# Hymba block on one core: split queries and keys stored interleaved, scan streams stored block by block, and a new order

## The chip, the cores and the metric

The kernel runs on one core of one Trainium2 chip. The metric is the device time of one execution in microseconds (us); less is better. Each core has a matrix engine (TensorE, PE in the profile), a vector engine (VectorE, DVE), an activation engine (ScalarE, ACT), a general engine (GpSimd, POOL), a queue engine that only issues transfers (SyncE, SP), and 16 DMA engines which all queues share. Transfers are issued here from SP, from POOL, and a few from ACT.

## The reference, cut to what matters

One layer over 1024 tokens of width 1024, all in float32: a SwiGLU FFN, a mixer, and a second FFN, each with a norm before and behind it. The mixer projects a token into an attention part and an RWKV part, computes both and projects their outputs back.

```python
f = _swiglu(_rmsnorm(h, ffn1_pre_g[l]), ffn1_w_gate[l], ffn1_w_up[l], ffn1_w_down[l])
h = h + 0.5 * _rmsnorm(f, ffn1_post_g[l])
z = _rmsnorm(h, mix_pre_g[l]) @ w_in[l]
y_att = _attention_group(z[..., :ATT_IN], cos, sin, attn_out_g[l])
y_rwkv = _rwkv7_group(z[..., ATT_IN:], ...)
mix = jnp.concatenate([y_att, y_rwkv], axis=-1) @ w_out[l]
h = h + _rmsnorm(mix, mix_post_g[l])
f = _swiglu(_rmsnorm(h, ffn2_pre_g[l]), ffn2_w_gate[l], ffn2_w_up[l], ffn2_w_down[l])
h = h + 0.5 * _rmsnorm(f, ffn2_post_g[l])
```

The attention has 8 heads of 64 features with rotary positions; each query sees three dilated windows of keys, (128, 1), (512, 4) and (2048, 16). The RWKV part has 8 heads; each runs a recurrence with a 64 x 64 state over the tokens, once forward and once backward, and the two results are added:

```python
sa = jnp.einsum('dbhvk,dbhk->dbhv', state, kk)
state = state * w[..., None, :] - sa[..., :, None] * kka[..., None, :] + v[..., :, None] * k[..., None, :]
y = jnp.einsum('dbhvk,dbhk->dbhv', state, r)
```

## The kernel before, in words

**Split numbers.** TensorE multiplies a rounded form of float32 (F32R) quickly. Where the kernel needs more precision it splits a value into a high part h and a low part l (`split`: h by an ACT copy, l by a VectorE subtraction) and adds three or four products of parts.

**Stages.** FFN 1; projection of the low-rank inputs and the RWKV columns (`project_rwkv`, tiles zr); projection of keys, queries and values by tokens (`project_tokens`, tiles zq, in the order keys, queries, values); attention head by head (`attention`) mixed with the scan over 8 blocks of 128 tokens in both directions (`prep`, `solve`, `merge`, `chain`); the end of the mixer in 8 units (`finish_unit`) with the output projection; FFN 2. Nothing is held in the code's order: the whole program is recorded on a tape first, and the order is worked out for each engine (below).

**Queries and keys.** For each of 8 token tiles and each half of the heads, and for queries as for keys, `project_tokens` (L930) multiplies, rotates, and turns a [128, 2, 128] tile in PSUM (zt). ACT writes its high part (zth) and a full copy (zts), VectorE its low part (ztl); each has two buffers. Three POOL transfers put them into three DRAM tensors of [4 pairs of heads, 128, 1024]: q_d or kt_d, each with f, h and l. For a head, `stacked` (L1121) loads three tiles of 128 partitions with two half loads each (64 partitions): sq is query h over query l, kh is key h twice, kl is key l twice. `scores` inside `near` (L1142) adds sq x kh and sq x kl, which are the four products of parts. The full copies serve the widest window (`far`), a pair of heads at a time.

**Streams of the scan.** Decay and rate (w and a, one for each direction) come from `low_rank` (L997), the streams r, k, kk and v from `stream` (L1032). All lie in DRAM as [features / 128, 128, 1024]: a partition's 1024 tokens are one 4 KB row. `prep` (L1246) loads of each of them 128 tokens of all rows (tiles th_w, th_a and in3), forms the block's operands and writes the block's keys (d_kd) in the same layout; `chain` writes the block's outputs (d_y), from ACT's queue. `finish_unit` (L1442) loads 256 tokens of two rows of y and keys in both directions, r and v.

**Inverses.** `solve` (L1316) loads a block's matrix X from DRAM, runs 31 steps of two small operations (ttmp, Ti) on POOL for blocks 1 to 5 and on VectorE for the others, and stores the result (d_t, d_tt) from POOL; `merge` loads it back from POOL (tiles d, tt) for PE's products pa and pb.

**What sets the order.** `_Tape.cost` (L257) prices each operation: `took` is how long it holds its engine, `late` how long the result takes after that, `moved` the time on the DMA wire. `sweep` (L345) plays the program with these prices, engine by engine, always taking the ready operation of lowest rank; `order` (L460) runs sweeps forward and backward, keeps the best, then adds to the ranks of some ranges of operations the amounts of the table LEADS (45 entries) and sweeps once more. `play` (L486) issues the result; all operations therefore have L491 in the profile, and groups are told apart by the names of their tiles.

Of the kernel before, what the change touches and what calls it, by code (L numbers as in the profile page):

```python
# [11 lines left out]
F32 = mybir.dt.float32  # L12
F32R = mybir.dt.float32r
# [19 lines left out]
def _ap(src, off, pat):  # L33
# [66 lines left out]
class _Tape:  # L100
# [156 lines left out]
    def cost(self, op):  # L257
# [8 lines left out]
        if op.method == "dma_start":  # L266
            runs = [math.prod(q[1] for q in a.ap) // (a.ap[-1][1] if a.ap[-1][0] == 1 else 1) for a in (x, *op.ins)]
            size = math.prod(q[1] for q in x.ap) * 4
            half = any(a.tensor.name in self.home and a.ap[0][1] <= 64 for a in (x, *op.ins))
            op.took, op.late = (560 if op.eng == "gpsimd" else 360) + 200 * half, 1500 + (600 if half else 0)  # L270
            op.moved = (14 * max(runs) + 0.0384 * size) / 16
        elif op.eng == "tensor":
# [14 lines left out]
            op.late = 170  # L287
        elif op.eng == "vector":
# [8 lines left out]
            op.took, op.late = 150 + rate * n + (83 if "accum_out" in op.kwargs else 0), 35  # L297
            op.port = sum(self.home.get(a.tensor.name, (None,))[0].space is None for a in op.ins
                          if a.tensor.name in self.home and math.prod(q[1] for q in a.ap[1:]) > 1) > 1
            if op.method == "reciprocal":  # L300
                op.took = 150 + 5 * n
        elif op.eng == "scalar":
            func = op.args[2] if op.method == "activation" else None
            aps = sum(isinstance(op.kwargs.get(k), bass.AP) for k in ("scale", "bias"))
            op.took = 170 + 0.87 * n + 95 * aps + (188 if "accum_out" in op.kwargs else 0)
            op.load, op.late = LOADS.get(func, 0), 40
        else:
            op.took, op.late, op.port = (200 + 2.1 * n if op.method != "memset" else 130 + 0.8 * n), 40, op.method != "memset"

    def pace(self, last, op, idle):  # L310
# [4 lines left out]
        return took + 95 if last and last.grid != op.grid and idle < 100 else took  # L315

    def lag(self, p, s):

        if p.eng is None or p.eng == s.eng and p.method != "dma_start":
            return 0.0  # L320
        return p.late + p.moved + (200 if s.eng == "gpsimd" else 0)
# [23 lines left out]
    def sweep(self, back=False):  # L345
# [29 lines left out]
        follow, last, port = None, None, 0.0  # L375
        while True:
# [26 lines left out]
            while op is None and heap[e]:  # L403
# [5 lines left out]
                if tag:  # L409
# [5 lines left out]
                    if at > t + 1e-6:  # L415
                        push(later[e], (at, -op.rank, op.n, op))
                        op = None
                        continue
                    slots[tag].remove(at)
# [15 lines left out]
            if op.port:  # L435
                t = max(t, port)
                port = t + took
# [3 lines left out]
            if op.moved and not back:  # L441
                wire = max(wire, own) + op.moved
                end = wire - op.moved
            op.end = end
# [191 lines left out]
class _Kernel:  # L636
# [293 lines left out]
    def project_tokens(self, p, psum, x):  # L930

        nc, V, A, G, T = self.nc, self.nc.vector, self.nc.scalar, self.nc.gpsimd, self.nc.tensor
        for b, g in [(b, g) for b in (1, 0, 2) for g in range(2)]:
            hl = self.columns(p, b * 512 + g * 256, 256)
            for t in range(NT):
# [23 lines left out]
                for d, src in zip((self.q_d, self.kt_d)[b], (y, h, l)):  # L959
                    G.dma_start(d[g * 2:g * 2 + 2, :, ts].rearrange("a p t -> p a t"), src[:].bitcast(F32))  # L960
# [36 lines left out]
    def low_rank(self, ring, rows, psum, nm, y, reset):  # L997
# [6 lines left out]
        for d in range(2):  # L1004
# [11 lines left out]
            for pr in range(4):  # L1016
# [13 lines left out]
                self.nc.sync.dma_start(self.lr_d[nm][d][pr], o)  # L1030

    def stream(self, p, psum, ct, y):  # L1032
# [8 lines left out]
        elif ct < 4:  # L1041
            self.nc.gpsimd.dma_start(self.rk_d[ct], y)
        elif ct < 8:
            i = ct - 4
            self.nc.gpsimd.dma_start(self.rk_d[4 + i], y)
# [20 lines left out]
            self.nc.gpsimd.dma_start(self.rk_d[8 + i], kr)  # L1066
# [54 lines left out]
    def stacked(self, p, h):  # L1121

        ds = slice(h % 2 * 64, h % 2 * 64 + 64)
        (_, qh, ql), (_, kh, kl) = self.q_d, self.kt_d
# [8 lines left out]
    def near(self, psum, p, h, sq, kh, kl, v, far, between):  # L1133
# [8 lines left out]
        def scores(t):  # L1142
# [61 lines left out]
    def attention(self, psum, p):  # L1204
        X, F, ST = {}, {}, {}

        def load(pr):
# [7 lines left out]
            self.load(q, self.q_d[0][pr])  # L1215
            self.load(k, self.kt_d[0][pr])
# [29 lines left out]
    def prep(self, n, p, psum, big):  # L1246
# [4 lines left out]
        ls = slice(n * TB, (n + 1) * TB)  # L1251
# [3 lines left out]
        for d in range(2):  # L1255
            b = n if d == 0 else NC_ // BLK - 1 - n
            ts = slice(b * TB, (b + 1) * TB)
# [631 lines left out]
```

## Time and profile before

| | |
|---|---|
| median of 3 runs | 2257.74 us (2257.31 to 2260.61) |
| profiled execution | 2272.18 us, span 2270.4 us |
| PE busy | 2175.3 us, 96% of the span |
| VectorE, ACT, POOL busy | 1519.2, 1051.3, 720.1 us |
| mean granted PE clock | 0.970 |
| DMA | 408.71 MB, mean 180 GB/s |
| DMA pieces | 373,053, of which 279,282 are under 2 KB |

In the profile a row such as `kh<-d_kth SPq DMA_DIRECT2D` is a transfer into tile kh from DRAM tensor d_kth, issued by SP. Tensor and tile names are given without their numbers, so that in3 is shown as in, s12 as s and h1_d as d_h. A row of the table of stretches has the stretch, its length, then for PE, PE's weight loads, VectorE, ACT and POOL the busy time and in brackets the number of instructions, then PE's granted clock, the busy share of the 16 DMA engines, and GB/s. A PE that is busy at a granted clock of 0.5 works at half speed; busy time alone doesn't show it. In a table of single transfers the last number is the median time from issue to landing in us.

### The profile page before, as it was taken

To read this page: it belongs to the slowest core of one execution; us is meant where nothing else is said; L and a number is where in the kernel's file an instruction comes from. 1 tells how busy PE (TensorE), PEld (TensorE's weight loads), DVE (VectorE), ACT (ScalarE), POOL (GpSimd) and SP (SyncE) were. 2 spreads that over 40 slices of the span, in tenths; PEclk is the share of its full clock that TensorE was granted. 3 is DMA by queue.
4 is the path that set the end of the run, shared out by engine and by line. 5 is a ranking of instruction groups with operands and counts; after the bars stand their busy time and mean duration, and the time that the engine had idled before them with its cause. 6 is when DMAs were issued, how large, how long until landed. Compare 5 with 4: busy or idle time off the path is not lost.

```text
span 2270.4 us, 41200 instructions
## 1 busy us (share of the span) xinstructions
PE 2175.3 (96%) x15236; PEld 1799.2 (79%) x15236; DVE 1519.2 (67%) x2630; ACT 1051.3 (46%) x2023; POOL 720.1 (32%) x1038
## 2 busy tenths in 40 slices
PE   7999999999999999998989998898899999999998
PEld 5888888888887888898768777666688888888886
DVE  8877777775685477562635557647978777787566
ACT  6333333354576464543546566454533333335453
POOL 2244444520000010667373571221024444443000
PEclk9999999999999999999969799998999999999999
DMA  5355444586662377764967765587435544458665
GB/s 153 115 170 165 163 152 163 185 289 194 202 201 83 115 252 197 213 206 143 231 159 183 164 160 149 136 274 252 151 108 177 168 156 160 147 181 299 198 203 182
DMA packets 373053, 408.71 MB, mean 180 GB/s; under 512 B 76658, under 2 KB 279282, under 8 KB 372852
## 3 DMA queue, kind: packets, MB, share of 16 engines
q1 hardware_dynamic: 324096, 303.18, 45.2%
q0 software_dynamic: 30704, 94.44, 11.9%
q10 hardware_dynamic: 18052, 8.46, 1.4%
q8 instruction: 120, 1.97, 0.4%
q14 instruction: 81, 0.66, 0.1%
HBM read 271.69 MB, written 134.28 MB: 179 GB/s over the span
## 4 chain that ended last, share of the span: by engine, by line
PE 81%; DMA 6%; DVE 5%; POOL 2%; issue 2%; ACT 2%; SPq 1%; DVEq 0%; ACTq 0%; POOLq 0%
PE gu L491 37%; PE pd L491 17%; PE zr L491 5%; PE zq L491 5%; PE po L491 3%; PE pt L491 2%; PE lp L491 2%; DVE row L491 2%; PE s L491 2%; PE xu L491 2%; POOL Ti L491 1%; PE y L491 1%; POOL ttmp L491 1%; SPq L491 1%; DMA X<-d_x 1%
## 5 line engine op out<-in xcount | busy, mean ns | idle before, releaser
L491 ACT ACTIVATE wh<-raw 128x512 fp32r<-128x512 f32 x264 | 162.8, 628 | 373.5 <-PE gu L491 276.4
L491 POOL TENSOR_TENSOR row<-row 128x512 f32<-128x512 f32 x88 | 129.3, 1469 | 447.6 <-DVE row L491 420.2
L491 DVE TENSOR_TENSOR row<-gu,row 128x512 f32<-128x512 f32 x308 | 203.5, 685 | 101.1 <-PE gu L491 63.1
L491 DVE TENSOR_TENSOR wl<-raw,wh 128x512 fp32r<-128x512 f32 x264 | 214.5, 823 | 82.3 <-ACT wh L491 57.9
L491 PE MATMUL gu<-xh,wh 128*128 128x512 f32 x704 | 249.9, 394 | 3.6 <-ACT xh L491 1.5
L491 PE MATMUL gu<-xh,wl 128*128 128x512 f32 x704 | 250.6, 391 | 0.6 <-DVE wl L491 0.6
L491 PE MATMUL gu<-xl,wh 128*128 128x512 f32 x704 | 249.5, 393 | 0.0
L491 DVE TENSOR_TENSOR gwl<-graw,gwh 128x512 fp32r<-128x512 f32 (+1 forms) x176 | 116.4, 664 | 107.5 <-PE pd L491 76.0
L491 PE MATMUL pd<-gh,gwl 128*128 128x512 f32 x616 | 180.9, 391 | 0.5 <-DVE gwl L491 0.5
L491 PE MATMUL pd<-gl,gwh 128*128 128x512 f32 x616 | 180.0, 390 | 0.2 <-DVE gl L491 0.2
L491 PE MATMUL pd<-gh,gwh 128*128 128x512 f32 x616 | 180.2, 390 | 0.0
L491 ACT ACTIVATE gwh<-graw 128x512 fp32r<-128x512 f32 (+1 forms) x176 | 101.0, 577 | 137.0 <-PE pd L491 113.2
L491 PEld LDWEIGHTS gu<-xh,wh 128*128 128x128 f32 x704 | 132.9, 189 | 32.8 <-ACT xh L491 2.1
L491 PEld LDWEIGHTS gu<-xh,wl 128*128 128x128 f32 x704 | 132.3, 188 | 28.6 <-DVE wl L491 1.2
L491 PEld LDWEIGHTS gu<-xl,wh 128*128 128x128 f32 x704 | 132.6, 189 | 27.4 <-DVE xl L491 0.5
L491 PEld LDWEIGHTS pd<-gh,gwl 128*128 128x128 f32 x616 | 115.6, 188 | 25.3 <-DVE gwl L491 0.9
L491 PEld LDWEIGHTS pd<-gl,gwh 128*128 128x128 f32 x616 | 115.5, 188 | 24.7 <-DVE gl L491 0.6
L491 PEld LDWEIGHTS pd<-gh,gwh 128*128 128x128 f32 x616 | 115.5, 188 | 24.0
L491 ACT ACTIVATE gh<-raw 128x512 fp32r<-128x512 f32 x160 | 99.4, 629 | 57.0 <-PE pd L491 34.2
L491 DVE TENSOR_TENSOR gl<-raw,gh 128x512 fp32r<-128x512 f32 x160 | 115.7, 729 | 11.4 <-ACT gh L491 10.9
L491 POOL TENSOR_TENSOR ws<-ws 128x512 f32<-128x512 f32 x88 | 118.8, 1351 | 2.8
L491 POOL DMA_DIRECT2D d_hid<-row x154 | 83.8, 547 | 81.6 <-DVE row L491 67.6
(300 smaller groups left out, 5149.9 us busy)
## 6 DMA issues: line engine op xcount, KB each, us to landing
d_hid<-row POOLq DMA_DIRECT2D x154, 256.0 KB, 2.7
graw<-d_hid SPq DMA_DIRECT2D x132, 256.0 KB, 3.1
raw<-in_ffn_w_gate_dram SPq DMA_DIRECT2D x88, 256.0 KB, 3.0
raw<-in_ffn_w_up_dram SPq DMA_DIRECT2D x88, 256.0 KB, 3.1
ws<-in_ffn_w_down_dram SPq DMA_DIRECT2D x88, 256.0 KB, 3.7
d_ws<-ws POOLq DMA_DIRECT2D x88, 256.0 KB, 2.8
raw<-d_ws SPq DMA_DIRECT2D x88, 256.0 KB, 3.2
raw<-in_ffn_w_down_dram SPq DMA_DIRECT2D x66, 256.0 KB, 4.1
```

What stands on the lines that cost most here:

```text
L491: i = getattr(getattr(self.nc, op.eng), op.method)(*op.args, **op.kwargs).ins
```

## The change

**Interleaved split queries and keys.** The high and the low part are written into one tile w of [128, 2, 2, 128]. A new DRAM tensor kk holds, for each head, 64 features x (h, l) x 1024 tokens, so that 128 rows of 4 KB are one head. Queries have two such tensors: q1 with h before l, q2 with l before h. `stacked` loads three whole tiles for a head, and the scores are q1 x kk + q2 x kk: the same four products. A tile of keys now needs three POOL transfers (the full copy and two halves of w), a tile of queries five.

**Streams block by block.** w, a, the three streams, the written keys and the outputs lie in DRAM as [8 blocks, 128, rows, 128 tokens]. `prep` and `chain` move a partition's part of a block in one run; `low_rank` and `stream` write their 1024-token rows in 8 pieces of 128 tokens; `finish_unit` loads each stream but v in two transfers, since two blocks and two rows don't make one simple pattern.

**The order.** The prices of `cost`, the lags between operations and the pace of PE when its shape changes are other formulas; transfers have at most 8 in flight for each kind of queue in `sweep`; LEADS has 19 other entries. Every engine's order changes with that, also in the FFNs.

The diff, cut to its core (the new LEADS table is left out):

```diff
             size = math.prod(q[1] for q in x.ap) * 4
-            half = any(a.tensor.name in self.home and a.ap[0][1] <= 64 for a in (x, *op.ins))
-            op.took, op.late = (560 if op.eng == "gpsimd" else 360) + 200 * half, 1500 + (600 if half else 0)
-            op.moved = (14 * max(runs) + 0.0384 * size) / 16
+            rows = min(a.ap[0][1] for a in (x, *op.ins) if a.tensor.name in self.home)
+            op.took, op.late = 360 + 200 * (rows <= 64), 1700
+            if op.eng == "gpsimd":
+                op.took = 560 + 0.25 * max(runs)
+            runs = 6 * size / 4096 if op.eng == "gpsimd" else max(size / 4096, *runs)
+            op.moved = max((9.5 * runs + 0.0366 * size) / 16, size / (3.6 * rows))
...
-            op.late = 170
+            op.late = 200
...
-            op.took, op.late = 150 + rate * n + (83 if "accum_out" in op.kwargs else 0), 35
+            op.took, op.late = 68 + rate * n + 65 * (len(op.ins) > 2), 117
...
-            op.took = 170 + 0.87 * n + 95 * aps + (188 if "accum_out" in op.kwargs else 0)
-            op.load, op.late = LOADS.get(func, 0), 40
+            op.took, op.late = (68 if near else 111) + 0.833 * n + 90 * aps, 137
...
-        return took + 95 if last and last.grid != op.grid and idle < 100 else took
+        if last and last.grid != op.grid:
+            took += 95 * (idle < 100) + 100 * (op.grid == (128, 128) and op.args[1].dtype == F32R)
+        return took
...
+                if op.moved and not back and lanes[e == "gpsimd"][0] > t + 1e-6:
+                    push(later[e], (lanes[e == "gpsimd"][0], -op.rank, op.n, op))
+                    op = None
+                    continue
...
-                y, h, l = (p.tile([128, 2, 128], dt, name="z" + n, tag="z" + n, bufs=2)
-                           for n, dt in (("ts", F32), ("th", F32R), ("tl", F32R)))
+                y = p.tile([128, 2, 128], F32, name="zts", tag="zts", bufs=2)
+                w = p.tile([128, 2, 2, 128], F32R, name="zt", tag="zt", bufs=2)
+                h, l = w[:, :, 0], w[:, :, 1]
...
-                for d, src in zip((self.q_d, self.kt_d)[b], (y, h, l)):
-                    G.dma_start(d[g * 2:g * 2 + 2, :, ts].rearrange("a p t -> p a t"), src[:].bitcast(F32))
+                G.dma_start((self.q_d, self.kt_d)[b][g * 2:g * 2 + 2, :, ts].rearrange("a p t -> p a t"), y)
+                for d, v in zip(self.qk_d[b], (w, w[:, :, ::-1])):
+                    for i in range(2):
+                        G.dma_start(_ap(d, (g * 512 + i * 256) * S + t * 128, [[2 * S, 128], [S, 2], [1, 128]]),
+                                    v[:, i].bitcast(F32))
...
-                self.nc.sync.dma_start(self.lr_d[nm][d][pr], o)
+                self.nc.sync.dma_start(self.blocked(self.lr_d[nm][d], pr), o.rearrange("p (n t) -> p n t", t=TB))
+
+    def blocked(self, dst, j):
+        return dst[:, :, j, :].rearrange("n p t -> p n t")
...
-            self.nc.gpsimd.dma_start(self.rk_d[ct], y)
+            self.nc.gpsimd.dma_start(self.blocked(self.rk_d, ct), y.rearrange("p (n t) -> p n t", t=TB))
...
-        for nm, parts in (("sq", (qh, ql)), ("kh", (kh, kh)), ("kl", (kl, kl))):
+        for nm, src in zip(("q1", "q2", "kk"), (*self.qk_d[0], *self.qk_d[1])):
             t = p.tile([128, S], F32R, name=nm, tag=nm)
-            for j, src in enumerate(parts):
-                self.load(t[j * 64:j * 64 + 64].bitcast(F32), src[h // 2, ds, :])
+            self.load(t[:].bitcast(F32), _ap(src, h * 128 * S, [[S, 128], [1, S]]))
...
-                T.matmul(ps[:, :e - c], sq[:, qs], kh[:, k0 * 128 + c:k0 * 128 + e], start=True, stop=False)
-                T.matmul(ps[:, :e - c], sq[:, qs], kl[:, k0 * 128 + c:k0 * 128 + e], start=False, stop=True)
+                T.matmul(ps[:, :e - c], q1[:, qs], k[:, k0 * 128 + c:k0 * 128 + e], start=True, stop=False)
+                T.matmul(ps[:, :e - c], q2[:, qs], k[:, k0 * 128 + c:k0 * 128 + e], start=False, stop=True)
...
-                self.load(th[nm], self.lr_d[nm][d][:, :, ls].rearrange("a p t -> p a t"))
+                self.load(th[nm], self.lr_d[nm][d][n])
...
-            self.load(x3.rearrange("p j a t -> p (j a) t"), self.rk_d[:, :, ts].rearrange("a p t -> p a t"))
+            self.load(x3.rearrange("p j a t -> p (j a) t"), self.rk_d[b])
...
-            self.nc.sync.dma_start(self.kd_d[d][:, :, ls].rearrange("a p t -> p a t"), kd)
+            self.nc.sync.dma_start(self.kd_d[d][n], kd)
...
-            self.nc.scalar.dma_start(self.y_d[d][:, :, ls].rearrange("a p t -> p a t"), YB[d])
+            self.nc.scalar.dma_start(self.y_d[d][n], YB[d])
...
-            self.load(z[nm], src[ps2, :, sl].rearrange("a p t -> p a t"))
+            for j in range(2):
+                self.load(z[nm][:, j, :].rearrange("p (n t) -> p n t", t=TB),
+                          src[o * nb:(o + 1) * nb, :, 2 * g + j, :].rearrange("n p t -> p n t"))
```

More of the change, by code (lines that the diff above doesn't have):

```diff
@@ L296, in cost @@
                 rate = 2.1
-            op.took, op.late = 150 + rate * n + (83 if "accum_out" in op.kwargs else 0), 35
+            op.took, op.late = 68 + rate * n + 65 * (len(op.ins) > 2), 117
+            if "accum_out" in op.kwargs:
+                op.took, op.late = op.took + 8, 227
             op.port = sum(self.home.get(a.tensor.name, (None,))[0].space is None for a in op.ins
@@ L300, in cost @@
             if op.method == "reciprocal":
-                op.took = 150 + 5 * n
+                op.took = 68 + 5 * n
+            op.took += 110 * (x.ap[0][1] <= 64)
         elif op.eng == "scalar":
@@ L304, in cost @@
             aps = sum(isinstance(op.kwargs.get(k), bass.AP) for k in ("scale", "bias"))
-            op.took = 170 + 0.87 * n + 95 * aps + (188 if "accum_out" in op.kwargs else 0)
-            op.load, op.late = LOADS.get(func, 0), 40
-        else:
-            op.took, op.late, op.port = (200 + 2.1 * n if op.method != "memset" else 130 + 0.8 * n), 40, op.method != "memset"
+            near = all(self.home.get(a.tensor.name, (None,))[0].space == PSUM for a in op.ins[:1] if a.tensor.name in self.home)
+            op.took, op.late = (68 if near else 111) + 0.833 * n + 90 * aps, 137
+            if "accum_out" in op.kwargs:
+                op.took, op.late = op.took + 100, 230
+            op.took += 110 * (x.ap[0][1] <= 64)
+            op.load = LOADS.get(func, 0)
+        else:
+            op.took = 135 + 2.17 * n - min(n, 150) * 0.2 if op.method != "memset" else 110 + 0.8 * n
+            op.late, op.port = 134, op.method != "memset"
     def pace(self, last, op, idle):
@@ L314, in pace @@
             took /= 2
-        return took + 95 if last and last.grid != op.grid and idle < 100 else took
+        if last and last.grid != op.grid:
+            took += 95 * (idle < 100) + 100 * (op.grid == (128, 128) and op.args[1].dtype == F32R)
+        return took
     def lag(self, p, s):
-        if p.eng is None or p.eng == s.eng and p.method != "dma_start":
+        if p.eng is None or p.eng == s.eng == "tensor":
             return 0.0
-        return p.late + p.moved + (200 if s.eng == "gpsimd" else 0)
+        if p.eng != s.eng:
+            return p.late + p.moved + (200 if s.eng == "gpsimd" else 0)
+        if p.moved and s.moved and all(a.tensor.name != p.out[0].tensor.name for a in s.ins):
+            return 0.0
+        return p.late + p.moved
     def rate(self):
@@ L374, in sweep @@
                     push(later[op.eng], (0.0, -op.rank, op.n, op))
-        follow, last, port = None, None, 0.0
+        follow, last, port, lanes = None, None, 0.0, ([0.0] * 8, [0.0] * 8)
         while True:
@@ L436, in sweep @@
                 t = max(t, port)
-                port = t + took
+                port = t + took + 60
             op.start = t
@@ L1121, in stacked, with near @@
     def stacked(self, p, h):
-        ds = slice(h % 2 * 64, h % 2 * 64 + 64)
-        (_, qh, ql), (_, kh, kl) = self.q_d, self.kt_d
         out = []
-        for nm, parts in (("sq", (qh, ql)), ("kh", (kh, kh)), ("kl", (kl, kl))):
+        for nm, src in zip(("q1", "q2", "kk"), (*self.qk_d[0], *self.qk_d[1])):
             t = p.tile([128, S], F32R, name=nm, tag=nm)
-            for j, src in enumerate(parts):
-                self.load(t[j * 64:j * 64 + 64].bitcast(F32), src[h // 2, ds, :])
+            self.load(t[:].bitcast(F32), _ap(src, h * 128 * S, [[S, 128], [1, S]]))
             out.append(t)
         return out
-    def near(self, psum, p, h, sq, kh, kl, v, far, between):
+    def near(self, psum, p, h, q1, q2, k, v, far, between):
         nc, V, A, G, T = self.nc, self.nc.vector, self.nc.scalar, self.nc.gpsimd, self.nc.tensor
@@ L1214, in load @@
             q, k = (p.tile([128, S], F32, name=n, tag=n) for n in ("qp", "kp"))
-            self.load(q, self.q_d[0][pr])
-            self.load(k, self.kt_d[0][pr])
+            self.load(q, self.q_d[pr])
+            self.load(k, self.kt_d[pr])
             X[pr] = q, k, v3, vn
@@ L1256, in prep @@
             b = n if d == 0 else NC_ // BLK - 1 - n
-            ts = slice(b * TB, (b + 1) * TB)
             th = {}
@@ L1447, in finish_unit @@
         ps2, ts = slice(2 * g, 2 * g + 2), slice(b * FB, (b + 1) * FB)
-        back = slice(S - (b + 1) * FB, S - b * FB)
-        z = {}
-        for nm, src, sl in (("y0", self.y_d[0], ts), ("y1", self.y_d[1], back), ("k0", self.kd_d[0], ts),
-                            ("k1", self.kd_d[1], back), ("r", self.rk_d, ts), ("v", self.v_d, ts)):
+        nb, far, z = FB // TB, S // FB - 1 - b, {}
+        for nm, src, o in (("y0", self.y_d[0], b), ("y1", self.y_d[1], far), ("k0", self.kd_d[0], b),
+                           ("k1", self.kd_d[1], far), ("r", self.rk_d, b), ("v", None, 0)):
             z[nm] = p.tile([128, 2, FB], F32, name="f_" + nm, tag="f_" + nm)
-            self.load(z[nm], src[ps2, :, sl].rearrange("a p t -> p a t"))
+            if src is None:
+                self.load(z[nm], self.v_d[ps2, :, ts].rearrange("a p t -> p a t"))
+                continue
+            for j in range(2):
+                self.load(z[nm][:, j, :].rearrange("p (n t) -> p n t", t=TB),
+                          src[o * nb:(o + 1) * nb, :, 2 * g + j, :].rearrange("n p t -> p n t"))
         sg = p.tile([128, FB], F32, name="f_sg", tag="f_sg")
@@ L1582, in constants @@
         self.n3_d = [self.dram(f"n3{j}", [S, 66]) for j in range(2)]
[L1583 removed]
+        NB = NC_ // BLK
+        self.lr_d = {nm: [self.dram(f"{nm}{d}", [NB, 128, 4, TB]) for d in range(2)] for nm in "wa"}
         self.sg_d = self.dram("sg", [128, S])
[L1585 to L1587 removed]
+        self.rk_d, self.v_d = self.dram("rk", [NB, 128, 12, TB]), self.dram("v", [4, 128, S])
+        self.q_d, self.kt_d = (self.dram(nm, [4, 128, S]) for nm in ("qf", "kf"))
+        self.qk_d = [[self.dram(nm, [H, 64, 2, S]) for nm in nms] for nms in (("q1", "q2"), ("kk",))]
         self.vt_d = self.dram("vt", [2, S, 2, 4, 64])
[L1589 to L1590 removed]
+        self.kd_d = [self.dram(f"kd{d}", [NB, 128, 4, TB]) for d in range(2)]
+        self.y_d = [self.dram(f"y{d}", [NB, 128, 4, TB]) for d in range(2)]
         self.x_d, self.t_d, self.tt_d = ([self.dram(f"{n}{j}", [r, w]) for j in range(4)]
```

16 lines of the change are left out of this document (6 added, 10 removed), and 14 rows, old and new, of the table LEADS.

## The prediction

> **What bounds the kernel now.** I read the page first, then the busy times by stretch, then the chain of waits inside the stretches where TensorE (PE) is not full.
>
> ```profile
> span 2270.4 us, 41200 instructions
> PE 2175.3 (96%) x15236; PEld 1799.2 (79%) x15236; DVE 1519.2 (67%) x2630; ACT 1051.3 (46%) x2023; POOL 720.1 (32%) x1038
> PE 81%; DMA 6%; DVE 5%; POOL 2%; issue 2%; ACT 2%; SPq 1%; DVEq 0%; ACTq 0%; POOLq 0%
> ```
>
> ```profile
> 0.00:660.00 660.00, 645.21 (x2860) 528.20 (x2861) 476.07 (x716) 279.04 (x479) 201.60 (x235) 1.00 0.55 178
> 660.00:900.00 240.00, 236.47 (x1317) 196.67 (x1315) 147.53 (x250) 142.20 (x265) 14.76 (x30) 1.00 0.54 171
> 900.00:1050.00 150.00, 145.90 (x1531) 139.86 (x1529) 86.25 (x217) 65.42 (x174) 100.04 (x170) 0.98 0.61 179
> 1050.00:1200.00 150.00, 128.89 (x1753) 108.10 (x1753) 63.51 (x149) 74.53 (x167) 80.14 (x175) 0.81 0.77 191
> 1200.00:1420.00 220.00, 205.25 (x3371) 170.00 (x3366) 141.08 (x352) 141.53 (x320) 93.77 (x180) 0.93 0.68 166
> 1420.00:1650.00 230.00, 202.70 (x1725) 152.58 (x1724) 159.89 (x307) 115.44 (x221) 39.72 (x40) 0.93 0.64 201
> 1650.00:2270.40 620.40, 610.87 (x2698) 503.74 (x2696) 444.82 (x643) 233.11 (x400) 190.13 (x209) 1.00 0.55 181
> ```
>
> After the times of a row come the granted clock, the DMA share and GB/s. The two FFNs (to 660, from 1650) have a full PE at clock 1.00 and hold nothing that the change touches; nor does the RWKV projection (660 to 900) leave more than 3.5 us. What can be won lies from 900 to 1650: PE idles 4.1, 21.1, 14.8 and 27.3 us there, 67 in all, and the clock takes (1 - 0.98) x 150 = 3, then 28.5, 15.4 and 16.1, some 63 us of PE's speed. The worst stretch is 1050 to 1200, where attention and scan blocks share the engines and DMA is busiest (0.77). Its chain names the DMAs:
>
> ```profile
> by line: POOL Ti L491 11.8%; POOL ttmp L491 11.1%; PE zq L491 9.1%; issue 6.7%; DMA X<-d_x 6.5%; PE lp L491 6.3%; DMA in<-d_rk 6.2%; DMA d<-d_t 6.1%; PE xu L491 5.8%; SPq L491 3.8%; PE s L491 3.8%; PE pa L491 2.6%; DMA d_x<-lm 2.1%; DMA d_n
> 1093.91 9.26 DMA in<-d_rk
> 1109.27 5.50 DMA X<-d_x
> 1171.28 6.14 DMA d<-d_t
> ```
>
> ```profile
> by line: PE s L491 14.0%; PE lp L491 11.0%; PE pt L491 10.6%; PE po L491 9.6%; PE y L491 6.6%; PE st L491 5.6%; issue 5.4%; PE xu L491 5.3%; DMA X<-d_x 3.7%; PE bp L491 3.3%; POOL Ti L491 3.2%; POOL ttmp L491 3.1%; ACT e L491 1.4%; DMA wor<
> 1302.10 8.12 DMA X<-d_x
> ```
>
> So 6.5 + 6.2 + 6.1 + 2.1 = 20.9% of 150 us and 3.7% of 220 us, about 39.5 us of the path from 1050 to 1420, are four small transfers of the scan blocks. Why they are slow stands in SP's queue:
>
> ```profile
> 1083.33 0.67 SPq L491 DMA_DIRECT2D sq<-d_qh  x1
> ...
> 1085.42 1.24 SPq L491 DMA_DIRECT2D kh<-d_kth  x2
> 1086.70 1.24 SPq L491 DMA_DIRECT2D kl<-d_ktl  x2
> ...
> 1088.61 0.43 SPq L491 DMA_DIRECT2D kp<-d_ktf  x1
> ...
> 1090.58 3.22 SPq L491 DMA_DIRECT2D sv<-d_vt  x2
> 1093.91 0.53 SPq L491 DMA_DIRECT2D in<-d_rk  x1
> ```
>
> Half-tile loads of the attention go out at 0.62 us each, the queue fills, two small loads take 3.22 us to issue, and the block's streams (in) go behind them. The rates below are of stretches in which nearly all traffic was of one shape: 512-byte pieces, 1 KB pieces, 2 KB pieces, 4 KB rows over 128 partitions, and 4 KB rows into 64 partitions.
>
> ```profile
> 1100.00:1103.00 3.00, 3.00 (x40) 1.86 (x38) 0.00 (x0) 1.94 (x4) 0.00 (x0) 1.00 1.19 300
> 1479.00:1482.00 3.00, 3.00 (x26) 2.46 (x21) 0.63 (x1) 0.59 (x1) 2.46 (x2) 1.00 1.09 384
> 484.50:486.00 1.50, 1.50 (x8) 1.23 (x8) 0.69 (x1) 1.29 (x3) 0.00 (x0) 1.00 1.05 393
> 828.00:831.00 3.00, 3.00 (x15) 2.49 (x14) 1.08 (x4) 2.96 (x7) 0.18 (x1) 1.00 1.02 418
> 1087.00:1092.00 5.00, 5.00 (x51) 4.74 (x50) 2.59 (x5) 0.00 (x0) 0.00 (x0) 0.50 1.06 250
> ```
>
> **The change part by part.** Sizes and counts:
>
> ```profile
> in<-d_rk SPq DMA_DIRECT2D x16, 768.0 KB, 6.0
> d_w<-ra SPq DMA_DIRECT2D x8, 512.0 KB, 3.6
> kh<-d_kth SPq DMA_DIRECT2D x16, 256.0 KB, 5.5
> f_k<-d_kd SPq DMA_DIRECT2D x16, 256.0 KB, 5.4
> d_qh<-zth POOLq DMA_DIRECT2D x16, 128.0 KB, 3.4
> d_rk<-us POOLq DMA_DIRECT2D x8, 512.0 KB, 3.5
> ```
>
> A, stacked loads: per head six of 256 KB into 64 partitions become three of 512 KB into 128; 8 heads, 12.58 MB. At 250 GB/s that was 50.3 us of DMA, at 418 it is 30.1: 20.2 less. SP issues 48 x 0.62 = 29.8 us before and 24 x 0.43 = 10.3 after. The score matmuls stay as many.
>
> B, block streams: per block and direction, w, a, the three streams and the written keys are 4 x 512-byte or 12 x 512-byte pieces a partition and become rows of 2 or 6 KB; with y 29.4 MB. At 300 GB/s 97.9 us, at 384 (the lower of the two longer shapes) 76.5: 21.4 less.
>
> Of A all, and of B 11 of 16 loads, 14.7 us, fall in 1050 to 1420, where DMA was busy 0.77 x 150 + 0.68 x 220 = 265 us: 34.9, or 13% less. On the 39.5 us of chain that is 5.1 us if landings shrink in proportion; if they shrink as the slowest does to its median (9.26 to 6.0, 35%) it is 13.9, and nothing if their cost is latency alone. I take 9, the middle, since the queue's own delay shrinks too. SP's share of the chain, 3.8% of 150 = 5.7 us, falls with 0.62 to 0.43: 2. Idle time that goes gives back clock: 11 of 35.9 us idle against 43.9 us of clock loss would be 13.5 at most; I take 3, as shortened waits mostly still end a busy phase. Together -14, between -33 and 0.
>
> C, the writes of the split: a key tile has three POOL issues as before, a query tile five instead of three, so 32 more and 4.19 MB more (14.0 us at 300 GB/s).
>
> ```profile
> L491 POOL DMA_DIRECT2D d_tt<-X x16 | 13.2, 823 | 24.1 <-DVE X L491 18.8 <-DMA d_t<-Ti 3.5 <-issue 1.7
> L491 POOL DMA_DIRECT2D d_qf<-zts x16 | 11.6, 724 | 0.4 <-ACT zts L491 0.3
> L491 POOL DMA_DIRECT2D d_rk<-us x8 | 4.3, 542 | 62.5 <-DVE zl L491 32.1 <-DVE us L491 11.4 <-issue 8.1
> ```
>
> ```profile
> 970.00:1070.00 100.00, 94.78 (x836) 92.87 (x832) 44.00 (x100) 36.04 (x98) 72.54 (x134) 0.98 0.55 162
> ```
>
> That is 32 x 0.724 = 23.2 us on POOL, which in the query stage has 27.5 of 100 us free between the solves of two blocks. Behind each write on POOL stand the solve's next step and the reload of inverses (d<-d_t) for which PE waits; behind the tile's two buffers stand ACT's next split and PE's next rotation. Bounds 0 and +23; since it fits, but with 4 us to spare, I take +5.
>
> D, the 28 whole-row stores (16 of w and a, 8 + 4 of the streams) are cut into 512-byte pieces: 14.7 MB, 35.1 us at 418, 48.9 at 300, 13.8 more; POOL up to 12 x (0.823 - 0.542) = 3.4. The cover is PE in 660 to 900 (236.5 of 240 us) at a DMA share of 0.54; taken as 0, and +14 if block 0 waits for the last store.
>
> E, the end: eight units load five streams in two pieces of 512-byte runs where one of 1 KB runs did: 40 more issues (17.2 us of SP at 0.43) and 10.5 MB at 300 for 384 GB/s, 7.7 us. DMA there is 0.64 busy, and PE idles 27.3 us already; bounds 0 and +17, taken as +3.
>
> F, the order. Prices, lags and lead times of the planner change, so every engine's order changes. Its old table gives a VectorE operation of 512 elements 150 + 532 = 682 ns, its new one 600. Back to back they start 0.60 us apart, though each shows 0.69:
>
> ```profile
> 470.11 0.69 DVE L491 TENSOR_TENSOR gl<-raw,gh 128x512 fp32r<-128x512 f32 x1
> 470.71 0.69 DVE L491 TENSOR_TENSOR gwl<-graw,gwh 128x512 fp32r<-128x512 f32 x1
> ```
>
> Its old price of a half-tile load is (14 x 64 + 0.0384 x 262144) / 16 = 685 ns, 383 GB/s, where the row above has 250; the new one is 1138 ns, 230 GB/s. The new prices are nearer in both; that the order built on them is better doesn't follow, for it also drops the old lead times. Bounds: half of the 67 us idle gone (-34), or one more stretch as bad as 1050 to 1200 (+21). Bringing that stretch half-way to its neighbour's idle (14.75 x 150/220 = 10.1 for 21.1) gives 5.5 us and half-way to its clock (0.81 to 0.87) 9; less what A and B already have there, I take -11.
>
> Sum: -14 + 5 + 0 + 3 - 11 = -17. The profiled execution took 2272.2 us (span 2270.4), 14.4 above the median of the runs, 2257.7; so about 2255 profiled and **2241** timed. DMA time in total falls by only 20.2 + 21.4 - 14.0 - 13.8 - 7.7 = 6.1 us: the gain, if any, is in where it falls.
>
> By a rule of the Trainium skill (DMA: Bandwidth & Descriptors, Specifications) transfers of 512 bytes already run at line rate, so whole rows would be worth nothing. The rows of 300 against 384 and 393 GB/s say otherwise. By that rule B, D and E's bytes fall away, A and B's -14 keeps A's part, -8, E keeps +2, and the sum is -12, 2246.
>
> **The rivals.**
> 1. POOL becomes the bound at the end of the query stage (970 to 1070): 72.5 + 23.2 is 95.7 of 100 us, so waits of more than 4.3 us inside it move the first scores and the second block's inverses. It decides once the solves of two blocks stay in that stage. For it: d<-d_t already lands on the chain. Against: attention needs only the last writes. Price +23 and no gain from the order: 2257.7 - 14 + 23 + 3 = 2270, slower.
> 2. The new order is worse: one more stretch of 21 us idle, and the layout worth 6: 2273.
> 3. The DMAs were hidden: the landings are latency, the order a wash, C and E small: 2258.
> 4. The order fills half the idle time (-34) and the loads bring their 14, less 8: 2218.
>
> **How the numbers follow.** Forecast 0.43 (its own range 2225 to 2253), rival 4 0.15, rival 3 0.13, rival 1 0.12, rival 2 0.17. A measurement tells about 0.2%, 4.5 us. Faster 0.58, same 0.13, slower 0.29. The range 2208 to 2272 takes in the forecast, rivals 1, 3 and most of 4, and leaves the far half of rival 2 and the bounds added up.
>
> **What would show it.** A: kh and kl gone, SP issues of the new loads near 0.43 us, and stretches of them near 400 GB/s. B: in<-d_rk landing below 6.0 us and gone from the chain near the start of attention. C: POOL over 90 of 100 us in the query stage (rival 1), with waits of PE for DMA d or of ACT for the tile's writes. E: more idle after 1420. F: idle and clock in 1050 to 1420 changed by more than 20 us. The prediction is wrong if DMA rows leave the chain and the time stays, or if PE's idle time merely moves past 1420.

## The result and the profile after

| | before | after |
|---|---|---|
| median | 2257.7 us (2257.3 to 2260.6) | 2242.4 us (2240.2 to 2248.1) |
| ratio, 95% interval | | 0.9933, 0.9912 to 0.9954 |
| profiled execution | 2272.2 us | 2243.9 us |
| mean granted PE clock | 0.970 | 0.981 |

The kernel became 15.3 us faster. The two profiled executions differ by 28.3 us, 13 more, because that of before lay 14.4 us above its median and that of after only 1.5; so no single stretch may be read to better than some ten microseconds. The page of the changed kernel, with its chain of waits:

```profile
span 2242.1 us, 41288 instructions
PE 2151.9 (96%) x15236; PEld 1782.4 (79%) x15236; DVE 1533.2 (68%) x2630; ACT 1045.2 (47%) x2023; POOL 737.6 (33%) x1070
PE 74%; DMA 9%; DVE 8%; POOL 4%; issue 3%; ACT 2%; SPq 0%; DVEq 0%; ACTq 0%; POOLq 0%
```

The busy times by stretch of the changed kernel, with the columns of the table shown for before (the end of the mixer now lies at 1630):

```profile
660.00:900.00 240.00, 235.10 (x1269) 193.32 (x1268) 144.86 (x234) 141.49 (x269) 18.87 (x30) 0.99 0.56 169
900.00:1050.00 150.00, 142.63 (x1555) 137.17 (x1554) 90.88 (x242) 68.58 (x178) 111.58 (x179) 1.00 0.69 211
970.00:1070.00 100.00, 96.60 (x907) 94.17 (x906) 42.49 (x96) 33.58 (x92) 84.97 (x152) 1.00 0.61 187
1050.00:1200.00 150.00, 133.18 (x2006) 113.47 (x2006) 73.73 (x180) 83.53 (x193) 82.47 (x182) 0.92 0.72 211
1200.00:1420.00 220.00, 213.49 (x3460) 176.92 (x3457) 146.38 (x389) 146.91 (x319) 106.41 (x206) 0.96 0.63 174
1420.00:1630.00 210.00, 189.31 (x1491) 145.50 (x1490) 148.05 (x259) 103.67 (x203) 33.50 (x30) 0.92 0.65 204
```

From 1050 to 1420 PE idles 16.8 + 6.5 = 23.3 us, where it idled 35.9, and the clock takes 0.08 x 150 + 0.04 x 220 = 20.8 us, where it took 43.9. Past 1420 it idles 20.7, where it idled 27.3. The query stage idles a little more, 7.4 for 4.1. So most of the gain shows where the scan blocks and the attention share the engines, as idle time and as clock together.

The chain of waits of the changed kernel inside 1050 to 1200 (start, length, what):

```profile
1074.78 9.10 DMA d<-d_t
1142.50 6.46 DMA th_w<-d_w
```

Its transfers (size, median us from issue to landing), and SP's queue during one head's loads of queries and keys:

```profile
in<-d_rk SPq DMA_DIRECT2D x16, 768.0 KB, 5.7
q<-d_q SPq DMA_DIRECT2D x16, 512.0 KB, 6.3
kk<-d_kk SPq DMA_DIRECT2D x8, 512.0 KB, 5.5
```

```profile
1226.85 0.43 SPq L509 DMA_DIRECT2D q<-d_q  x1
1227.37 0.38 SPq L509 DMA_DIRECT2D kk<-d_kk  x1
1227.81 0.42 SPq L509 DMA_DIRECT2D q<-d_q  x1
```

Of the 24 loads of queries and keys, 22 are issued in 0.32 to 0.43 us each. The load of the three streams (in) has gone from the chain near the start of attention. In its place stand the reload of inverses with 9.10 us and the block's decay (th_w), whose rows are just as whole now: the chain as a whole names DMA for 9% where it named 6%. The median landing of in fell from 6.0 to 5.7 us, no more, and further on the load still stands on the chain, with 7.67 us:

```profile
1250.72 7.67 DMA in<-d_rk
```

The faster time therefore doesn't yet say that the layout brought it.

### The profile page after: what moved, and what is told of

Read it like the earlier page. It is cut to its first block, busy times and chain, and to the rows that moved or that the text cites. A ratio compares the mean times of both kernels' runs of the same rounds, so it can differ in the third digit from the quotient of the medians.

```text
span 2242.1 us, 41288 instructions
## 1 busy us (share of the span) xinstructions
PE 2151.9 (96%) x15236; PEld 1782.4 (79%) x15236; DVE 1533.2 (68%) x2630; ACT 1045.2 (47%) x2023; POOL 737.6 (33%) x1070
## 3 DMA queue, kind: packets, MB, share of 16 engines
q0 software_dynamic: 32240, 98.64, 12.4%
## 4 chain that ended last, share of the span: by engine, by line
PE 74%; DMA 9%; DVE 8%; POOL 4%; issue 3%; ACT 2%; SPq 0%; DVEq 0%; ACTq 0%; POOLq 0%
PE gu L509 34%; PE pd L509 18%; PE zr L509 6%; DVE row L509 2%; PE pt L509 2%; PE s L509 2%; PE po L509 2%; PE lp L509 2%; PE zq L509 1%; DVE wl L509 1%; PE xu L509 1%; POOL d_q L509 1%; PE y L509 1%; POOL Ti L509 1%; PE st L509 1%
## 5 line engine op out<-in xcount | busy, mean ns | idle before, releaser
L509 DVE TENSOR_TENSOR wl<-raw,wh 128x512 fp32r<-128x512 f32 x264 | 233.3, 898 | 75.2 <-PE gu L509 40.1
L509 POOL TENSOR_TENSOR row<-row 128x512 f32<-128x512 f32 x88 | 122.2, 1389 | 394.7 <-DVE row L509 350.0
L509 PE MATMUL gu<-xh,wl 128*128 128x512 f32 x704 | 238.7, 391 | 0.5 <-DVE wl L509 0.5
L509 PE MATMUL gu<-xh,wh 128*128 128x512 f32 x704 | 235.6, 393 | 3.7 <-ACT wh L509 1.8
L509 PE MATMUL gu<-xl,wh 128*128 128x512 f32 x704 | 235.0, 392 | 0.0
L509 PE MATMUL pd<-gl,gwh 128*128 128x512 f32 x616 | 185.3, 391 | 0.5 <-DVE gl L509 0.5
L509 PE MATMUL pd<-gh,gwh 128*128 128x512 f32 x616 | 185.0, 391 | 0.4 <-ACT gh L509 0.4
```

The costliest lines, as they stand in the source:

```text
L509: i = getattr(getattr(self.nc, op.eng), op.method)(*op.args, **op.kwargs).ins
```

## The experiments

The change has two halves that can be taken apart: the layout (steps A to E of the prediction) and the order (F). The theory on record is the prediction's sum; its rival is that the layout is worth nothing or less and the order everything. To hold the order still, I computed the order of every instruction from one kernel's planner and gave it as a fixed list to a kernel with another layout. A transfer that replaces others stands at the place of the first of them on its queue, writes at the last; some places had to move for a dependency. The traces bear out that the order was held: by the names of the tiles, ACT and POOL compute in the same sequence as in the kernel that gave the list, VectorE too but for 32 operations on renamed tiles, and PE but for at most 10 of 15,236. "Old order" and "new order" below mean these lists. Ratios are to the kernel before, measured beside each kernel on the same chip. Three chips were used; the medians of before on them were 2258.8, 2260.8 and 2259.8 us. A ratio is therefore the safer number where two kernels come from different chips. The profile of a kernel is one execution of it and can lie off its median: the one of the split in the old order lies 7.8 us below, those of the split in the new order and of the old layout with new engine prices 5.3 and 8.6 us above.

**Layout and order apart.** The changed kernel's code in the old order, and the old kernel's code in the new order:

```diff
-        k.nc.play(k.nc.order())
+        k.nc.play(k.nc.given())     # the list made from the other kernel's order
```

> The whole change of layout (split queries and keys interleaved, streams block by block), but every instruction in the order of the kernel before: a transfer that replaces others stands in the place of the first of them on its queue (writes: of the last). No planner's order, so what is seen is the layout alone. The prediction's theory: -14 + 5 + 0 + 3 = -6 us, about 2252. Rival 'the order did it': 2256 to 2262, no gain. Rival 'the layout did it': 2240 to 2246, as fast as the whole change.

> The old layout, but every instruction in the order of the changed kernel (half loads both in the place of the whole load). Theory: part F alone, -11, about 2247. Rival 'the order did it': 2240 to 2245. Rival 'the layout did it': 2256 to 2260. A third possibility: the new order counts on the faster loads and is worse than the old one without them, above 2262; then layout and order are worth something only together.

Measured: the layout in the old order 2272.3 us, 1.0053 (1.0033 to 1.0073), which is slower; the old layout in the new order 2240.6 us, 0.9915 (0.9894 to 0.9937), which is as fast as the whole change. The layout alone costs 12 us by the ratio and 13.5 by the medians, and the order alone brings 19 or 18. The stretches of the old layout in the new order:

```profile
1050.00:1200.00 150.00, 138.39 (x1918) 118.22 (x1916) 72.03 (x174) 82.08 (x190) 77.22 (x171) 0.85 0.79 204
1200.00:1420.00 220.00, 210.71 (x3399) 174.13 (x3399) 143.92 (x374) 143.86 (x313) 109.55 (x213) 0.97 0.70 174
```

PE idles 11.6 + 9.3 = 20.9 us here instead of 35.9, and the clock takes 29.1 instead of 43.9, with the half-tile loads, the 512-byte pieces and a DMA share of 0.79 (before: 0.77) all in place. So that DMA load alone did not make this stretch slow. The load of the streams (in) is gone from the chain between 1050 and 1200 here too, though its layout is the old one, and it stands there later, as long as in the changed kernel:

```profile
1256.49 7.33 DMA in<-d_rk
```

**The two halves of the layout, in the old order.** Only the interleaved split (A and C), and only the streams by blocks (B, D and E):

```diff
 # split_in_old_order: streams as before            # blocks_in_old_order: q, k as before
-        self.rk_d, self.v_d = self.dram("rk", [NB, 128, 12, TB]), self.dram("v", [4, 128, S])
+        self.rk_d, self.v_d = self.dram("rk", [12, 128, S]), self.dram("v", [4, 128, S])
...
-        self.q_d, self.kt_d = (self.dram(nm, [4, 128, S]) for nm in ("qf", "kf"))
-        self.qk_d = [[self.dram(nm, [H, 64, 2, S]) for nm in nms] for nms in (("q1", "q2"), ("kk",))]
+        self.q_d, self.kt_d = ([self.dram(f"{nm}{c}", [4, 128, S]) for c in "fhl"]
...
```

(The first edit belongs to the one, the second to the other; both are against the changed kernel, and cut to the tensors' shapes.)

> Only the interleaved split queries and keys (parts A and C), in the order of before. Theory: A's share of the -14, by its 20.2 of 34.9 us of DMA, is -8, and C +5: 2255. Rival 1 of the prediction (POOL is the bound at the end of the query stage): -8 + 23, about 2273. If the order itself shields it (POOL has slack): 2250.

> Only the block by block streams (parts B, D and E), in the order of before. Theory: B -6, D 0, E +3: 2255. By the skill's line-rate rule for 512 bytes, B and E's bytes are worth nothing and only the 40 further issues count: 2258 to 2260. If E or D is on the path: above 2262.

Measured: the split 2265.5 us, 1.0025 (1.0008 to 1.0041); the streams 2263.4 us, 1.0023 (1.0005 to 1.0040). Each is a little slower alone, and the two together, 0.48%, come near the 0.53% of both. For the streams, the stretches, a transfer and a group of POOL's issues of that kernel:

```profile
660.00:900.00 240.00, 236.86 (x1309) 196.57 (x1308) 147.45 (x248) 142.73 (x265) 19.08 (x30) 0.99 0.56 171
1050.00:1200.00 150.00, 130.79 (x1826) 110.91 (x1824) 66.29 (x155) 76.09 (x169) 80.05 (x175) 0.83 0.73 195
1200.00:1420.00 220.00, 204.07 (x3338) 167.66 (x3336) 149.46 (x386) 144.99 (x325) 94.56 (x182) 0.95 0.67 173
```

```profile
in<-d_rk SPq DMA_DIRECT2D x16, 768.0 KB, 5.6
```

```profile
L497 POOL DMA_DIRECT2D d_rk<-us x8 | 7.2, 895 | 60.0 <-DVE zl L497 31.4 <-DVE us L497 11.0 <-ACT zh L497 7.1
```

The DMA share falls by 0.04 of 150 and 0.01 of 220 us, about 8 us of DMA time, and PE's idle time stays: 19.2 + 15.9 = 35.1 us, where it was 35.9. The clock takes 36.5 us here where it took 43.9, but the profile of before is the slower execution of the two by 10 us, while by the medians this kernel is the slower one. The saved DMA time is real, and no gain of time follows from it; what B alone is worth, without D and E, no run measures. The cut stores cost POOL 895 ns instead of 542, and PE stays full there (236.9 of 240).

**The second copy of the queries, in the old order.** The split without C: the queries are written once, and the second tile is loaded from that copy with its high and low rows swapped:

```diff
-        self.qk_d = [[... for nms in (("q1", "q2"), ("kk",))]
+        self.qk_d = [[... for nms in (("q1",), ("kk",))]
...
-        for nm, src in zip(("q1", "q2", "kk"), (*self.qk_d[0], *self.qk_d[1])):
+        for nm, src in (("q1", _ap(qd, at, [[S, 128], [1, S]])), ("q2", _ap(qd, at + S, [[2 * S, 64], [-S, 2], [1, S]])),
+                        ("kk", _ap(kd, at, [[S, 128], [1, S]]))):
```

> Part A without part C (queries stored once, the swapped tile loaded from the same copy; streams in the old layout), in the order of the kernel before. Theory now: A alone is worth 12 us in any order, about 2247, and then C costs 2265.5 - 2247 = 18 in the old order, not the +5 of the prediction. If A is worth something only in the new order: 2256 to 2262, and C then costs 4 to 9.

Measured: 2252.4 us, 0.9963 (0.9948 to 0.9977). So A alone brings 7.4 us in the old order (8 by the ratio), and C takes 13 (2265.5 - 2252.4; by the ratios 0.62%, 14). Where C's time goes shows in the last query matmul (zq) and the first score matmul (s<-kk,q). The columns end with the first and the last start; before, then with two copies, then with one:

```profile
L491 PE MATMUL zq<-zl,xh x384: 274/283/415, 880.8 to 1063.3; 128*128 128x256 f32 x192
```

```profile
L497 PE MATMUL zq<-zl,xh x384: 274/283/420, 882.5 to 1081.5; 128*128 128x256 f32 x192
...
L497 PE MATMUL s<-kk,q x192: 220/397/796, 1112.0 to 1381.0; 128*128 128x512 f32 x96, 128*128 128x128 f32 x64, 128*128 128x384 f32 x32
```

```profile
L497 PE MATMUL zq<-zl,xh x384: 275/283/416, 880.1 to 1068.1; 128*128 128x256 f32 x192
...
L497 PE MATMUL s<-kk,q x192: 220/397/796, 1098.3 to 1373.3; 128*128 128x512 f32 x96, 128*128 128x128 f32 x64, 128*128 128x384 f32 x32
```

The query stage ends 13.4 us later with the second copy, and the first score starts 13.7 us later. What ACT waited for from 970 to 1085 (total, times, longest), first with two copies, then with one:

```profile
ACT zt L497 <- DMA d_q<-zt: 22.5, 5, 5.5
```

```profile
ACT zt L497 <- DMA d_q<-zt: 12.4, 5, 4.7
```

ACT's next split needs one of the two buffers of zt, and that is free only when its last write has landed; with four writes of a query tile instead of two this wait grows by 10.1 us. Over these 100 us POOL, which issues the writes, seems to have room in the kernel with two copies:

```profile
970.00:1070.00 100.00, 91.20 (x768) 88.16 (x768) 43.81 (x104) 31.10 (x89) 82.40 (x143) 0.97 0.58 174
```

But its idle time lies ahead of 1021. From 1022 to 1076 POOL never waits longer than 0.44 us, and the chain of waits runs along it. The chain from 1020 to 1075 by line, before, with two copies, with one; and the first step of the solve and the first store of its inverses, with two copies and with one:

```profile
by line: PE zq L491 78.5%; DMA d<-d_t 5.4%; PE pa L491 3.5%; POOL d_va L491 3.0%; issue 2.7%; PE lp L491 2.1%; PE bp L491 1.4%; PE zt L491 1.2%; POOL d L491 1.0%; POOL d_qh L491 0.7%; POOL d_ql L491 0.5%; POOL d_qf L491 0.3%
by line: POOL d_q L497 31.1%; POOL Ti L497 21.3%; POOL ttmp L497 20.1%; issue 9.5%; POOL d_va L497 8.5%; POOL d_qf L497 6.7%; PE zq L497 0.9%; DVE zt L497 0.8%; ACT zts L497 0.7%; PE zt L497 0.4%; POOLq L497 0.3%; ACT zt L497 0.0%; ACTq L49
by line: issue 19.3%; PE zq L497 15.3%; POOL d_va L497 13.2%; POOL Ti L497 11.1%; POOL ttmp L497 9.8%; POOL d_q L497 9.3%; DMA d<-d_t 7.5%; POOL d_qf L497 5.3%; POOL d_t L497 2.4%; POOL d_tt L497 2.0%; ACT zz L497 1.6%; POOL d L497 1.0%; PE
```

```profile
1018.68 0.23 POOL L497 TENSOR_TENSOR ttmp<-X,Ti 128x31 f32<-128x31 f32 x1
1075.77 0.78 POOL L497 DMA_DIRECT2D d_t<-Ti  x1 [0.30 <-POOL Ti L497]
...
1010.15 0.44 POOL L497 TENSOR_TENSOR ttmp<-X,Ti 128x31 f32<-128x31 f32 x1
1059.01 0.78 POOL L497 DMA_DIRECT2D d_t<-Ti  x1 [0.65 <-POOL Ti L497]
```

With two copies POOL's writes and solve steps are 31.1 + 21.3 + 20.1 + 8.5 + 6.7 = 87.7% of the chain, where with one copy the same five are 48.7% and before PE's query matmuls lead with 78.5%. The solve starts 8.5 us later and stores its inverses 16.8 us later, and PE waits for their reload. So about half of the delay arises ahead of the solve, where by their waits ACT stands for a free buffer and POOL for ACT, and the other half behind its start, where the added writes stand in POOL's full queue between its steps. The price is that of the late buffer and of the busy engine together; how it divides rests on these two profiles. Of the 13.4 us only 5.8 are left at the end of these two executions (2257.7 and 2251.9), since that of the split lies below its median. The whole layout in the old order shows the same delay: its first score starts at 1110.7, that of the streams alone at 1091.5.

**The same pieces in the new order.** Old streams with one copy, and old streams with two:

> Streams in the old layout; queries and keys interleaved, but the second copy of the queries (low part first) is never written: its tile is loaded from the first copy with the two rows of each feature swapped by the load's source pattern. So part A without part C, 32 POOL transfers and 4.19 MB of writes fewer than the change, in the order of the changed kernel. Beside the old layout in the new order (2240.6): if A is worth its -8, 2232; if the new order has hidden the half loads already, 2239 to 2242; if loads with swapped rows are slow, above 2243.

> Parts A and C (second query copy written by POOL), streams in the old layout, in the order of the changed kernel. Beside the kernel with one query copy (2228.0) it prices C, beside the changed kernel (2242.4) the blocks, both in the new order. Theory: C costs 12 to 16 there too, 2240 to 2244, and the blocks are worth nothing. Rival: the new order was planned with the five writes and hides them, 2228 to 2232; then it is the blocks that cost 10 to 14.

Measured: 2228.0 us, 0.9858 (0.9823 to 0.9892), and 2233.6 us, 0.9880 (0.9860 to 0.9900). Along the new order the time goes 2240.6 (nothing of the layout), 2228.0 (A), 2233.6 (and C), 2242.4 (and B, D, E): -12.5, +5.6, +8.8 by the medians, and -13, +5, +12 by the ratios. The intervals of the first and the last step are apart, the first barely; that of C is not, so C's price in the new order is not shown. The query stage ends 1.8 us later there with the second copy (1071.2 against 1069.4). The version with one copy beats both kernels. Its swapped load is the third row here (SP's queue of that kernel):

```profile
1289.13 0.34 SPq L497 DMA_DIRECT2D q<-d_q  x1
1289.57 0.79 SPq L497 DMA_DIRECT2D kk<-d_kk  x1
1290.40 0.56 SPq L497 DMA_DIRECT2D q<-d_q  x1
```

In all eight heads it is issued in 0.55 to 0.57 us; the plain load in its place in the kernel with two copies takes 0.32 to 0.43. So it costs SP some 0.2 us a head more.

Part of what the streams cost may lie at the end of the mixer. From the last y matmul of the scan to the last output matmul (op), first the changed kernel, then the split in the new order without the streams:

```profile
L509 PE MATMUL op<-wol,xh x64: 387/389/799, 1508.4 to 1578.2; 128*128 128x512 f32 x64
...
L509 PE MATMUL y<-lm,uv x512: 222/222/369, 956.3 to 1491.6; 128*64 128x64 f32 x171
```

```profile
L497 PE MATMUL op<-wol,xh x64: 387/392/800, 1507.7 to 1575.1; 128*128 128x512 f32 x64
...
L497 PE MATMUL y<-lm,uv x512: 221/222/369, 956.5 to 1492.5; 128*64 128x64 f32 x171
```

That is 86.6 us with the streams by blocks and 82.6 without, 4 us that may belong to the 40 more loads; these two executions differ by 4.9 us as a whole. In the old order the same stretch takes 86.6 us with the streams by blocks and 85.7 before, only 0.9 more. The rest of the 8.8 us, and the 5 us in the old order, I could not place in a stretch: single profiles scatter by more.

**What in the order brought the time.** The planner's prices and lags, its prices of transfers with a limit on those in flight, and the table of lead times changed together. Four kernels without lead times:

```diff
-LEADS = ((2346, 2471, -8761), (2786, 2996, 7847), ...)
+LEADS = ()
```

> The changed kernel with an empty table of lead times: new layout, new prices, the plain order of the sweeps. If the prices make the gain of the order (theory now: the 18 us of part F come from prices nearer to the chip), it stays within 5 us of the changed kernel, 2240 to 2248. If the new lead times make it, it is above 2256.

> The kernel before with an empty table of lead times: old layout, old prices. If the old lead times are worth something, above 2265, by as much as they were worth; if lead times move little, 2255 to 2262. Together with the next kernel it prices the formulas alone.

> Old layout, planned with the new prices, no lead times: against the kernel before without lead times only the prices differ. Prices theory: 10 us or more below that kernel, and near 2240 to 2250. Lead-times theory: within 5 us of that kernel.

The fourth has the change's prices and lags for the engines, but prices transfers as the old planner does and knows no limit in flight:

```diff
-            op.took, op.late = 150 + rate * n + (83 if "accum_out" in op.kwargs else 0), 35
+            op.took, op.late = 68 + rate * n + 65 * (len(op.ins) > 2), 117
...
             half = any(a.tensor.name in self.home and a.ap[0][1] <= 64 for a in (x, *op.ins))
...
             op.moved = (14 * max(runs) + 0.0384 * size) / 16
```

> Old layout, no lead times, planned with the new prices and lags of the engines (VectorE, ACT, POOL, PE) but the old prices of transfers and without the limit of transfers in flight. Between the old prices (2282.8) and all new ones (2238.7): if the engines' prices make the 44 us, 2238 to 2248; if the transfers' prices do, 2275 to 2285; shared, about 2260.

Measured, all without lead times:

| | median | ratio, interval |
|---|---|---|
| new layout, new prices | 2247.0 | 0.9937, 0.9915 to 0.9959 |
| old layout, old prices | 2282.8 | 1.0100, 1.0069 to 1.0131 |
| old layout, new engine prices | 2270.2 | 1.0050, 1.0032 to 1.0068 |
| old layout, all new prices | 2238.7 | 0.9906, 0.9881 to 0.9930 |

The new lead times are worth nothing that can be told (0.9937 against 0.9933); the old ones were worth some 22 us (2282.8 against 2260.8). Without lead times, prices of the engines bring 12.6 us over the old prices, and prices of transfers with the limit in flight 31.5 more (11 and 33 by the ratios). Which of the last two does it, the prices or the limit, no run separates. The last stretch of the mixer shows part of it; old prices, new engine prices, all new prices:

```profile
1420.00:1640.00 220.00, 186.05 (x1590) 141.97 (x1589) 135.20 (x246) 98.86 (x196) 32.20 (x30) 0.89 0.64 202
```

```profile
1420.00:1640.00 220.00, 182.49 (x1593) 135.06 (x1593) 137.76 (x250) 100.14 (x196) 33.63 (x34) 0.88 0.62 195
```

```profile
1420.00:1640.00 220.00, 198.42 (x1555) 153.22 (x1554) 163.31 (x277) 108.69 (x212) 34.59 (x33) 0.96 0.63 201
```

PE idles 34.0, 37.5 and 21.6 us of 220, at clocks of 0.89, 0.88 and 0.96: the second step shows here, the first does not. The executions profiled took 2282.3, 2278.9 and 2239.4 us, so the first step is only 3.4 us in them.

**One copy, planned for itself.** Old streams and one copy of the queries, with an order that the new prices make for this layout and no lead times:

> Part A without C, streams in the old layout, planned by the new prices for itself, no lead times. As the old layout planned for itself took 2238.7: with A's 12 about 2227. If the plan uses the freed POOL and SP time: 2218 to 2224. If plans for this layout scatter by more than that: 2230 to 2240.

Measured: 2240.4 us, 0.9898 (0.9877 to 0.9919). The same layout in the carried-over order took 2228.0. By the medians the two orders differ by 12 us on the same work, by the ratios by 9, with intervals that just overlap. Both come from the new prices; the carried-over one was made for the changed layout and has lead times. So the choice of the order moves the time about as much as a whole part of the layout does.

## Why the prediction was right

The time was right, 2241 for 2242.4, but two errors of opposite sign stand behind it, and that they cancel is luck. The sum gave the layout -6 (-14 + 5 + 0 + 3) and the order -11. The runs give the layout +2 by the medians and +4 by the ratios in the new order, neither clear of noise, and +12 to +14 in the old order; and they give the order -18.

- **A, the loads of whole tiles.** Its share was -8; it measured -7.4 in the old order and -12.5 in the new. The issues shrank as forecast, to about 0.4 us. Long stretches near 400 GB/s did not show, since other transfers ran beside the loads; the fastest of those looked at, 1269 to 1273, moved 376. Whether A's gain comes from fewer issues or from a faster transfer, no run separates. That the half loads moved 250 GB/s and whole rows 418 fits the Trainium skill (SBUF — State Buffer, "Door 1: The DMA port swizzle"), by which partitions 0 to 63 reach 8 of the 16 DMA ports and 0 to 127 all of them.
- **B, the block streams.** This step failed. "5.1 us if landings shrink in proportion", with the rest taken in the middle, assumed that a shorter piece of DMA time is a shorter landing. The median landing of in went from 6.0 to 5.6 us and idle time from 35.9 to 35.1: the lower bound that the step named itself, "nothing if their cost is latency alone". The row left the chain near the start of attention, as foretold, but it did so in the old layout with the new order as well, and it stands further on with 7.67 us in the new layout and 7.33 in the old: that sign told of the order, not of B. Nor does SP's queue explain all four slow transfers, since POOL issues the reload of inverses (d<-d_t). The Trainium skill's rule (DMA: Bandwidth & Descriptors, Specifications), by which 512-byte transfers already run at line rate, had the right consequence for the time, though not for the rates (300 against 384 and 393 GB/s).
- **C, the second copy.** Taken at +5 between 0 and +23, it cost 13 in the old order and 5.6 by the medians in the new, there within the noise. The error was "since it fits, but with 4 us to spare": the spare time lies ahead of 1021, and behind it POOL carries 87.7% of the chain, though over the whole 100 us it is busy for 82.4 and not for the feared 95.7. The prediction named the buffers too, and they make the first half of the delay (ACT waits 22.5 us for d_q<-zt against 12.4). In the new order PE is busy 96.6 of the same 100 us in the changed kernel, so the stage hardly gets longer.
- **D, the cut stores.** 0 fits: POOL's issues grew and PE stayed full. No run measures D alone.
- **E, the end.** +3 was taken; the time from the last y to the last output matmul grew by 0.9 us in the old order and 4.0 in the new, single profiles both. B, D and E together cost 5 in the old order and 9 to 12 in the new, where -3 was forecast (B's share of -6, and +3), and most of that has no place found.
- **F, the order.** The failing term is a size: "less what A and B already have there, I take -11". Nothing was to be deducted: the order brings its 18 without A and B, and A brings 12.5 on top of it; the half-way estimates ahead of the deduction (5.5 and 9) come nearer to the -18 measured. Idle time and clock in 1050 to 1420 did change by more than 20 us: 12.6 and 23.1 in the changed kernel, 15.0 and 14.8 with the old layout. That the old lead times would be missed was right (22 us), but the prices made good for more than that.
- **The rivals.** Rival 3 was right for the streams, whose saved DMA time brought nothing that shows, and wrong for the order and for A. Rival 1 was half right for C in the old order: POOL does become the bound at the end of the query stage, and the first scores and the next inverses come late; the buffers made the other half, and the price was 13 instead of 23. Rival 2 was wrong: the new order is the whole gain. Rival 4 named the right source, but not its size nor the loads' share.

## What to carry to other kernels

Where a kernel's order is planned, a change of layout comes with a new order, and their effects must be measured with the order held fixed: here two orders made with the same prices differ by 9 to 12 us on the same work, and the whole layout, which the total time seemed to praise, brought nothing that can be told in the new order and cost 12 to 14 us in the old. A saved DMA microsecond is a saving only if the landing that somebody waits for gets shorter; compare the median landing before and after, not the share of busy DMA. Before adding writes, count those that must land before a two-buffered tile is free again, and look where the issuing engine's free time lies: here one that was busy 82 of 100 us was still the bound in the second half of the window. A swapped source pattern at the load saved the added writes here, and that version took 2228.0 us.

## What the runs showed of the hardware

A load whose source runs through pairs of rows in swapped order into 128 partitions was issued in 0.55 to 0.57 us, where a plain one in its place took 0.32 to 0.43. SP took 0.55 to 0.60 us (medians) for a 256 KB load into 64 partitions in the kernel before and 0.36 to 0.38 for a 512 KB load into 128 in the changed one. Whole rows of 2 to 6 KB instead of 512-byte pieces took some 8 us off the DMA's busy time in 370 us, by the shares of two executions, and 0.4 us off the median landing of a 768 KB load. POOL's issue of the same 512 KB store took 542 ns as whole rows and 895 ns in 512-byte pieces.
